# Two transformer blocks on one core: S5 mixer output by channel in 32-row products, a stacked phase table, other convolution taps, banks and end

## The chip, the core and the metric

The kernel runs on one core of a Trainium2 chip. The time of a run is the device time of one launch in microseconds (us). TensorE (PE) multiplies, VectorE (DVE), ScalarE (ACT) and GpSimd (POOL) do the rest, SyncE (SP) issues the DMAs of the one queue in use here. PSUM is the memory into which PE writes; SBUF is the memory from which it reads.

## The reference, cut to what matters

Two blocks on 512 positions of width 1024. The first has an S5 state-space mixer, whose output goes through GELU and a gated linear unit, beside an attention mixer (called nsa), then a feed-forward part. The second has two more mixers and a feed-forward part with a 3x3 depthwise convolution; a last root-mean-square norm ends it.

```python
# S5 mixer: 32 groups of 16 channels, 64 complex states each
_, _, xr, xi = lax.associative_scan(combine, (a_seq_re, a_seq_im, bu_re, bu_im), axis=1)
y = (jnp.einsum('bsgp,gcp->bsgc', xr, c_re.astype(f32))
     - jnp.einsum('bsgp,gcp->bsgc', xi, c_im.astype(f32))
     + d_skip.astype(f32).reshape(SSM_GROUPS, SSM_GROUP) * ug).reshape(bsz, s, SSM_WIDTH)
yg = jax.nn.gelu(y)
out = yg * jax.nn.sigmoid(yg @ w_glu.astype(f32) + b_glu.astype(f32))
...
# second block's feed-forward part
u = _dwconv2d(h @ w_up, conv_w, rows, cols)
a, b = jnp.split(u, 2, axis=-1)
return (jax.nn.silu(a) * b) @ w_down
```

## The kernel before

**Products.** Every large fp32 product is made of three products of rounded halves (`mm3`, L210 to L212): high by high, high by low, low by high. A unit of a projection (`proj`) is a tile of 128 output rows by 512 positions, 24 matmuls for 1024 inputs, into one PSUM bank. ACT rounds a weight tile (`wh<-raw`), DVE or POOL makes its rest (`wl<-raw,wh`); buffers: raw 2, wh 3, wl 3.

**PSUM.** Tags `mm` (4 banks), `aux` (3), `sm` (1). A unit waits until a bank of its tag has been read out.

**Order.** A scheduler orders each engine's instructions when the kernel is built; on the chip each engine takes its own queue strictly in that order, and waits at an instruction whose inputs, bank or buffer are not there.

**S5.** The first four units of the first projection (the last is `ps_mm_275`) give the mixer's input, which goes through `uv` and 32 small DMAs into `ur`. The next 16 units (gates, `gt`) don't depend on the mixer: they are what PE can do while DVE computes it. `s5_half` runs for halves hf 0 and 1, each over two channel tiles jt (0, 1 and 2, 3):
- `products` forms s5A, s5B (input weights) and s5CAr, s5CAi (output weights) on DVE; PE transposes s5A and s5B (L696), ACT copies the result into s5W1r and s5W1i.
- Powers of the decay (the phases s5Pr, s5Pi) are made by doubling, up to 127 of them in 7 steps.
- L705, L706 and L709 make the kernel of the first four lags (s5KT, s5G); POOL adds the skip term, 10 DMAs spread it.
- L733 multiplies `ur` by s5W1; DVE turns the result by the phases, scans (L757), turns back (s5Xr, s5Xi).
- L770 and L772 give `py` (`ps_sm`): position by channel, four blocks. To come back to channel by position, hf 0 goes through ACT and 16 DMAs; jt 2 takes 16 ACT operations of 32 rows; jt 3 takes 8 of these, 8 DVE copies (L794) and one ACT operation. `yg` is the GELU's result, ysH and ysL its halves, the input of `glu`.

After `glu` follow nsa's projections. In nsa, L1097 and L1099 give scores, L1119 transposes, L1055 and L1137 serve the coarse branch (cX).

**Second feed-forward part.** `ffn2` projects 44 units. The first four run together (banks mm); `conv_psum` reads each unit from its bank: ACT makes the middle tap (caccf) and one more (ctapf), DVE adds seven taps one after the other, POOL adds ctapf. The bank is free after the last DVE tap. Units 4 to 21 have their wl from POOL.

**End.** The last eight units (wdn2c) update x; squares (nsq, ACT) are summed (nacc, DVE), summed over rows (L366), rv, rr (POOL), rdg (DVE), spread (L382), and 16 DVE operations write y, which 8 DMAs store; for positions 0 to 255 and then for 256 to 511.

Of the kernel before, what the change touches and what calls it, by code (L numbers as in the profile page):

```python
# [179 lines left out]
class Kern:  # L180
# [63 lines left out]
    def proj(self, aps, xs, cb, kt=8, first=0, le=None, order=None, tail=0, mid=None, halves=False,  # L244
             pre={}, mid0=None, mid_at=-2):
# [66 lines left out]
    def sumsq(self, x, tmp, sl, tags=("nsq", "nacc")):  # L312
        n = sl.stop - sl.start
        acc = None
        for k in range(8):
            sq = tmp.tile([128, n], F32, name="nsq", tag=tags[0], bufs=2)
            self.act(sq, x[k][:, sl], AF.Square)
            if acc is None:
                acc = sq
            else:  # L320
                a2 = tmp.tile([128, n], F32, name="nacc", tag=tags[1], bufs=2)
                self.tt(a2, acc, sq, OP.add)
                acc = a2
# [33 lines left out]
    def rstd(self, acc, n, width, root=False, between=None):  # L357
# [3 lines left out]
        pin = self.tc.keep_in_program_order if between else lambda i: i  # L361
        between = between or (lambda n: None)
        nb = n // 128
        ss = self.mmtile((128, 8), "sm")
        for j in range(nb):
            self.ss_turn = nc.tensor.matmul(ss[:, j:j + 1], acc[:, 128 * j:128 * j + 128], self.ones[:, :1], start=True,  # L366
                                            stop=True).ins.name
        between(2)
        v = self.sm.tile([128, 4], F32, name="rv", tag="rv", bufs=2)
        pin(self.ts(v[:, :nb], ss[:, :nb], 1.0 / width, OP.mult, EPS, OP.add))  # L370
# [7 lines left out]
        between(2)  # L378
        pin(self.tt(dg[:, :n].rearrange("p (b t) -> p b t", b=nb), self.ident[:, None, :].to_broadcast([128, nb, 128]),
                    r[:, :nb, None].to_broadcast([128, nb, 128]), OP.mult))  # L380
        rb = self.mmtile((128, 512), "mm" if root else "aux")
        nc.tensor.matmul(rb[:, :n], self.ones, dg[:, :n], start=True, stop=True)  # L382
        between(8)
# [204 lines left out]
    def s5(self, hp, p, hs, prm, xs, pre):  # L588
# [5 lines left out]
        uv1 = lambda: uv()[:, 0]  # L594
# [7 lines left out]
        def norm():  # L602
            r, self.rt = self.rstd(self.sumsq(xs, hp, full, ("yg", "glus")), T, D, root=True)
# [18 lines left out]
    def s5_half(self, hp, hf, A, Gp, m4, u4, s5d, ura, uv1):  # L622
# [16 lines left out]
        def products(o, g, x, last):  # L639
# [4 lines left out]
            for c in range(2):  # L644
                nc.gpsimd.memset(o[c], 0.0)
                U = tile([128, 8, 4, 16], "s5t", 1)
                V = self.mmtile((128, 512), "aux")
                self.tt(U, gb[0], xb[c], mul)
                self.tt(V.rearrange("p (a l c) -> p a l c", a=8, l=4), gb[1], xb[1 - c], mul)
# [12 lines left out]
        P = [tile([128, 8, 128], n) for n in ("s5Pr", "s5Pi")]  # L662
        nc.gpsimd.memset(P[0][:, :, 0:1], 1.0)
        nc.gpsimd.memset(P[1][:, :, 0:1], 0.0)
        self.ts(P[0][:, :, 1], u4[0][:, ps], 1.0, mul)
        self.ts(P[1][:, :, 1], u4[1][:, ps], 1.0, mul)
        n = 1
        while n < 128:

            m = min(n, 127 - n)  # L670
            if m > 0:
                sr = P[0][:, :, n:n + 1].to_broadcast([128, 8, m])
                si = P[1][:, :, n:n + 1].to_broadcast([128, 8, m])
                xr, xi = P[0][:, :, 1:m + 1], P[1][:, :, 1:m + 1]
                orr, oi = P[0][:, :, n + 1:n + m + 1], P[1][:, :, n + 1:n + m + 1]
# [50 lines left out]
        for jt in (2 * hf, 2 * hf + 1):  # L726
            ur = ura[:, jt]
            q4 = slice(4 * (jt % 2), 4 * (jt % 2) + 4)
            wr = self.mmtile((128, 512), "aux")
            wi = self.mmtile((128, 512), "aux")  # L730
# [69 lines left out]
    def glu(self):  # L800
# [16 lines left out]
        for k in range(4):  # L817
            y = ys[k // 2][:, k % 2]
# [830 lines left out]
    def conv_psum(self, ps, w, pool, tag, bufs, tbufs):  # L1649
# [17 lines left out]
        self.tt(av[:, 1:8], av[:, 1:8], tv[:, 0:7], OP.add, nc.gpsimd)  # L1667
# [427 lines left out]
```

## Time and profile before

| what | value |
|---|---|
| median of 3 runs | 1656.02 us (1654.74 to 1656.45) |
| the profiled execution | 1655.87 us |
| its span, first to last instruction | 1654.2 us |
| mean granted clock of PE | 0.973 of full speed |
| busy in the span: PE, DVE, ACT, POOL | 1571.7, 1155.2, 733.0, 399.6 us |

Shares of the span are averages over stages that wait for different things; what counts for an engine is where it waits. A busy PE may run at half speed: the granted clock tells. Half of full speed is 1.2 GHz, full speed 2.4 GHz.

### The profile page before, as it was taken

Reading aid. Unit: us, or ns where it says so; the run is one execution under the profiler, and the core shown is the slowest. Engines: PE = TensorE matmul, PEld = TensorE weight load, DVE = VectorE, ACT = ScalarE, POOL = GpSimd, SP = SyncE. Lnnn points to the kernel's source line nnn. Section 1 sums busy time; section 2 is a strip of 40 time slices with the busy share of each in tenths; the row PEclk is TensorE's granted clock in tenths of the full one; section 3 lists DMA queues with packets and bytes.
Section 4 is the critical chain, followed back from the end, with each engine's and each line's share of the span. In section 5 each row is a group of like instructions: output and inputs, shape, how many; then the busy total and the mean of one; then the engine's idle time right before and its main releaser. Section 6 shows DMA issues by size and latency. Waiting matters only on the chain.

```text
span 1654.2 us, 22302 instructions
## 1 busy us (share of the span) xinstructions
PE 1571.7 (95%) x8277; PEld 1308.7 (79%) x8277; DVE 1155.2 (70%) x2209; ACT 733.0 (44%) x1286; POOL 399.6 (24%) x355
## 2 busy tenths in 40 slices
PE   7998898899999999999999999989989899999997
PEld 5887676677898888888887888878879788888886
DVE  8988625675769854863538888577868798777755
ACT  4354426553444213352335555556554454343422
POOL 1100203222100000000012222315220566656552
PEclk9999897999999999999999999999999899999998
DMA  5331310003346763733212011111212223233322
GB/s 178 105 96 47 124 59 26 14 20 98 126 166 206 249 218 110 250 124 102 83 64 65 26 39 52 59 52 51 77 52 69 72 94 102 90 102 91 101 86 80
DMA packets 60268, 158.34 MB, mean 96 GB/s; under 512 B 12416, under 2 KB 20352, under 8 KB 60032
## 3 DMA queue, kind: packets, MB, share of 16 engines
q1 hardware_dynamic: 60160, 156.92, 29.9%
q8 instruction: 65, 1.06, 0.3%
q14 instruction: 43, 0.35, 0.1%
HBM read 152.57 MB, written 2.10 MB: 94 GB/s over the span
## 4 chain that ended last, share of the span: by engine, by line
PE 73%; DVE 10%; ACT 5%; issue 2%; POOL 1%; DMA 0%; POOLq 0%; DVEq 0%; ACTq 0%
PE ps_mm L210 21%; PE ps_mm L211 21%; PE ps_mm L212 21%; PE ps_sm L1130 2%; PE ps_mm L1119 1%; DVE caccm L200 1%; DVE wl L191 1%; ACT L188 1%; DVE hgE L191 1%; PE ps_aux L1573 1%; DVE caccf L200 1%; PE ps_aux L1097 1%; ACT wh L188 0%; PE ps_mm L1007 0%; DVE hgl L1486 0%
## 5 line engine op out<-in xcount | busy, mean ns | idle before, releaser
L188 ACT ACTIVATE wh<-raw 128x1024 fp32r<-128x1024 f32 (+3 forms) x234 | 236.7, 1012 | 536.2 <-PE ps_mm L211 415.7
L191 DVE TENSOR_TENSOR wl<-raw,wh 128x1024 fp32r<-128x1024 f32 (+2 forms) x162 | 198.0, 1223 | 115.3 <-ACT wh L188 108.2
L200 DVE SCALAR_TENSOR_TENSOR caccf<-ps_mm,cwf,caccf 128x441 f32<-128x441 f32 (+2 forms) x308 | 206.7, 694 | 34.5 <-ACT ctapf L188 28.8
L191 POOL TENSOR_TENSOR wl<-raw,wh 128x1024 fp32r<-128x1024 f32 (+2 forms) x72 | 159.8, 2221 | 168.0 <-ACT wh L188 167.1
L210 PE MATMUL ps_mm<-h4H,wh 128*128 128x512 f32 (+1 forms) x368 | 137.0, 380 | 7.8 <-DVE caccf L200 7.6
L212 PE MATMUL ps_mm<-h4H,wl 128*128 128x512 f32 (+1 forms) x368 | 138.3, 378 | 0.0
L211 PE MATMUL ps_mm<-h4L,wh 128*128 128x512 f32 (+1 forms) x368 | 138.3, 379 | 0.0
L191 POOL TENSOR_TENSOR rr<-rv,nhalf 128x2 f32<-128x2 f32 x9 | 8.7, 968 | 435.0 <-DVE rv L197 435.0
L210 PE MATMUL ps_mm<-h2H,wh 128*128 128x512 f32 (+1 forms) x280 | 103.8, 372 | 0.0
L212 PE MATMUL ps_mm<-h2H,wl 128*128 128x512 f32 (+1 forms) x280 | 103.6, 371 | 0.0
L211 PE MATMUL ps_mm<-h2L,wh 128*128 128x512 f32 (+1 forms) x280 | 103.6, 371 | 0.0
L210 PE MATMUL ps_mm<-aH,wh 128*128 128x512 f32 (+1 forms) x272 | 102.6, 377 | 0.5 <-DVE x L191 0.5
L212 PE MATMUL ps_mm<-aH,wl 128*128 128x512 f32 (+1 forms) x272 | 102.7, 378 | 0.0
L211 PE MATMUL ps_mm<-aL,wh 128*128 128x512 f32 (+1 forms) x272 | 102.4, 377 | 0.0
L210 PE MATMUL ps_mm<-hH,wh 128*128 128x512 f32 x224 | 89.5, 406 | 9.6 <-ACT hH L188 8.9
L1265 DVE CUSTOM_DVE_ANT_0 msc<-wmod,cB,cols 128x1024 bf16<-128x1024 f32 x64 | 82.0, 1281 | 21.2 <-DMA wmod<-in_wmod 20.8
L211 PE MATMUL ps_mm<-hL,wh 128*128 128x512 f32 x224 | 90.1, 403 | 0.0
L212 PE MATMUL ps_mm<-hH,wl 128*128 128x512 f32 x224 | 89.4, 400 | 0.0
L210 PEld LDWEIGHTS ps_mm<-h4H,wh 128*128 128x128 f32 x368 | 68.7, 190 | 21.1 <-issue 7.7
L211 PEld LDWEIGHTS ps_mm<-h4L,wh 128*128 128x128 f32 x368 | 69.9, 190 | 13.2 <-DVE h4L L200 0.4
L212 PEld LDWEIGHTS ps_mm<-h4H,wl 128*128 128x128 f32 x368 | 69.8, 190 | 13.1
L210 PE MATMUL ps_mm<-faH,wh 128*128 128x512 f32 (+1 forms) x194 | 72.4, 373 | 0.0
(521 smaller groups left out, 4040.9 us busy)
## 6 DMA issues: line engine op xcount, KB each, us to landing
raw<-in_wup SPq DMA_DIRECT2D x76, 512.0 KB, 3.4
wmod<-in_wmod SPq DMA_DIRECT2D x48, 512.0 KB, 4.3
raw<-in_wdn SPq DMA_DIRECT2D x32, 512.0 KB, 3.5
raw<-in_win SPq DMA_DIRECT2D x28, 512.0 KB, 3.4
raw<-in_wout SPq DMA_DIRECT2D x8, 512.0 KB, 3.4
raw<-in_wdn2a SPq DMA_DIRECT2D x8, 512.0 KB, 3.4
raw<-in_wdn2b SPq DMA_DIRECT2D x8, 512.0 KB, 3.4
raw<-in_wdn2c SPq DMA_DIRECT2D x8, 384.0 KB, 3.0
```

Of the source, the lines that this page charges most:

```text
L188: return self.nc.scalar.activation(o, i, f, **k)
L191: return (e or self.nc.vector).tensor_tensor(o, a, b, op)
L200: return self.nc.vector.scalar_tensor_tensor(o, a, s, b, op0, op1)
L210: mm(ps, wh, xh, start=start, stop=False)
L211: mm(ps, wh, xl, start=False, stop=False)
L212: mm(ps, wl, xh, start=False, stop=stop)
L1097: nc.tensor.matmul(S[:, :n2], self.qs[:, 2 * j + g, c], self.ks[:, 2 * br + g, :n2], start=True, stop=False)
L1119: nc.tensor.transpose(tp[:, 128 * b:128 * b + 128], P[g, i][:, 128 * b:128 * b + 128], self.ident)
L1130: nc.tensor.matmul(O[64 * g:64 * g + 64, 128 * i:128 * i + 128], self.V[:, b, c:c + 64], PT[g][:, 128 * b:128 * b + 128], start=br == 0 an ...
L1265: ins = nc.vector.tensor_tensor_reduce(sc, w, cB[:, c], 1.0, bm[:, m:m + 1], OP.mult, OP.add, acc)
L1573: nc.tensor.matmul(ps[:, j], EE[:, li, 128 * j:128 * j + 128], vw(EE[:, li])[:, j], start=True, stop=True)
```

## The change

The mixer, the second feed-forward part and the end are written in another way; no weight layout changes.

1. **S5.** In `products` the last operation is one DVE instruction of 128 rows into PSUM, and ACT copies it out in two 64-row halves (before: two DVE instructions of 64 rows). The phases stand in one tile s5P, real and imaginary side by side, and a doubling step takes 4 DVE instructions, two of them of double width, instead of 6. The wr and wi of odd jt take `mm` banks instead of `aux`. The output `py` is made by 48 products of 32 rows per jt, four side by side (`tile_position`), instead of 12 of 128 rows; it comes out by channel, and one ACT operation makes yg. The copies and 32 DMAs behind it are gone.
2. **Second feed-forward part.** Units 0 to 17 have two taps on ACT and POOL and six on DVE. Units 4 and 5 get a bank of aux and the bank of sm.
3. **End.** wdn2c runs as 5 + 3 units; the squares of x tiles 0 to 4 are summed ahead of the last three, and L366's successor sums two accumulators. Of y, two tiles of eight are made by ACT and POOL.

```diff
-            ps = self.mmtile()
+            ps = self.mmtile(tag=banks[i - first] if i - first < len(banks) else "mm")
...
+                last[c](V, U, V)
                 for h in range(2):
                     r = slice(64 * h, 64 * h + 64)
-                    d = o[c][r, :, :, 16 * h:16 * h + 16].rearrange("p a l c -> p (a l) c")
-                    u = U[r].rearrange("p a l c -> p (a l) c")
-                    v = V[r].rearrange("p (n c) -> p n c", c=16)
-                    last[c](d, u, v)
+                    self.act(o[c][r, :, :, 16 * h:16 * h + 16].rearrange("p a l c -> p (a l) c"),
+                             V[r].rearrange("p (n c) -> p n c", c=16))
...
-                t = tile([128, 8, 64], "s5pt")[:, :, :m]
-                self.tt(t, xi, si, mul)
-                self.tt(orr, xr, sr, mul)
-                self.tt(orr, orr, t, sub)
-                t = tile([128, 8, 64], "s5pt")[:, :, :m]
-                self.tt(t, xi, sr, mul)
-                self.tt(oi, xr, si, mul)
-                self.tt(oi, oi, t, add)
+                by = lambda c: PP[:, c:c + 1, :, n:n + 1].to_broadcast([128, 2, 8, m])
+                x, o = PP[:, :, :, 1:m + 1], PP[:, :, :, n + 1:n + m + 1]
+                t = tile([128, 2, 8, 64], "s5pt")[:, :, :, :m]
+                self.tt(o, x, by(0), mul)
+                self.tt(t, x, by(1), mul)
+                self.tt(o[:, 0], o[:, 0], t[:, 1], sub)
+                self.tt(o[:, 1], o[:, 1], t[:, 0], add)
...
-            wr = self.mmtile((128, 512), "aux")
-            wi = self.mmtile((128, 512), "aux")
+            wr, wi = (self.mmtile((128, 512), ("aux", "mm")[jt % 2]) for _ in range(2))
...
-            for pl in range(4):
-                o = py[:, 128 * pl:128 * pl + 128]
-                pr = q4.start + pl
-                nc.tensor.matmul(o, G[:, pr].rearrange("p a b -> p (a b)"), ur[:, pl], start=True, stop=False)
-                for c in range(2):
-                    nc.tensor.matmul(o, CA[c][:, pr].rearrange("p a b -> p (a b)"), X[c][:, pl, 0:128],
-                                     start=False, stop=c == 1)
+            for st in range(4):
+                for i, (w, x) in enumerate(((G, ur), (CA[0], X[0]), (CA[1], X[1]))):
+                    for pl in range(4):
+                        nc.tensor.matmul(py[32 * pl:32 * pl + 32, 128 * st:128 * st + 128], w[:, q4.start + pl, st],
+                                         x[:, pl, 0:128], start=i == 0, stop=i == 2, tile_position=(0, 32 * pl))
...
+            self.act(yg.rearrange("p (c s) -> p s c", s=4), py.rearrange("p (s c) -> p s c", s=4), AF.Gelu_apprx_tanh)
...
-        self.act(tv[:, 0:7], rv[:, 0:7], scale=w[:, 1:2])
-        for dy, dx in ((1, 0), (0, -1), (0, 1), (-1, -1), (-1, 1), (1, -1), (1, 1)):
+        taps = ((0, -1), (0, 1), (-1, -1), (-1, 1), (1, -1), (1, 1), (1, 0), (-1, 0))
+        late = []
+        for i in range(8 - n_pool, 8):
...
+            self.act(g(t)[:, iy], rv[:, iy], scale=w[:, c:c + 1])
...
+        for dy, dx in taps[:8 - n_pool]:
...
+        for oy, t in late:
+            self.tt(av[:, oy], av[:, oy], t, OP.add, nc.gpsimd)
...
-                conv[m] = self.conv_psum(ps, cw[:, m // 2 + 22 * (m % 2)], p, "f", 8, 6)
+                conv[m] = self.conv_psum(ps, cw[:, m // 2 + 22 * (m % 2)], p, "f", 8, 6, 2 if m < 2 * lead else 1)
...
+                      banks=("aux", "sm"),
...
-            down("wdn2c", list(range(8)), 16, 6, tail=3, mid=lambda: rb.append(self.norm_factor(self.x, p, h0)))
+            down("wdn2c", list(range(5)), 16, 6)
+            for i, sl in enumerate((h0, h1)):
+                early.append(self.sumsq(self.x, p, sl, tags=("nsq", f"nacc{i}"), tiles=range(5)))
+            down("wdn2c", [5, 6, 7], 16, 6, tail=3, mid=mid)
```

In the changed kernel L687 is the transposes of s5A and s5B (before L696), L696, L697 and L700 the kernel of the first lags (before L705, L706, L709), L723 the product with `ur` (before L733), L761 the products for `py` (before L770, L772), L1101 the transposes of cX (before L1137). The order on PE, as built, moves in three places.

**PE behind the fourth unit `ps_mm_275`.** Before, two gate units (770, 803) stand between it and the first transposes of S5:

```order
L212 MATMUL ps_mm_275<-hH_78,wl_272 128x512
L210 MATMUL ps_mm_770<-hH_78,wh_766 128x512
...
L212 MATMUL ps_mm_803<-hH_78,wl_800 128x512
L696 MATMUL ps_aux_536<-ident_76,s5A_438 128x128 x4
L210 MATMUL ps_mm_803<-hH_78,wh_799 128x512
```

With the change, transposes, products with `ur` and the lag kernel come first, and the first gate unit is 786:

```order
L212 MATMUL ps_mm_275<-hH_78,wl_272 128x512
L687 MATMUL ps_aux_518<-ident_76,s5A_438 128x128 x4
L687 MATMUL ps_aux_524<-ident_76,s5A_438 128x128 x4
L687 MATMUL ps_aux_530<-ident_76,s5B_439 128x128 x4
L687 MATMUL ps_aux_536<-ident_76,s5B_439 128x128 x4
L723 MATMUL ps_mm_675<-ur_123,s5W1r_516 128x128 x4
L696 MATMUL ps_aux_543<-s5A_438,s5c_432 32x128
...
L697 MATMUL ps_aux_556<-s5B_439,s5nci_496 32x128
L723 MATMUL ps_mm_676<-ur_123,s5W1i_517 128x128 x4
L210 MATMUL ps_mm_786<-hH_78,wh_782 128x512
```

45 matmuls of gate units have moved from before the first transposes to behind the lag kernel.

**PE at the end of S5.** Before, the outputs of jt 3 (`ps_sm_1304`) come after the last gate unit (1575), among those of `glu` (1620 to 1622):

```order
L212 MATMUL ps_mm_1575<-hH_78,wl_1572 128x512
L210 MATMUL ps_mm_1620<-ysH_83,wh_1604 128x512
...
L770 MATMUL ps_sm_1304<-ur_123,s5G_1188 128x128
...
L772 MATMUL ps_sm_1304<-s5Xi_1295,s5CAi_1115 128x128
L210 MATMUL ps_mm_1620<-ysH_83,wh_1604 128x512
```

With the change, jt 3 (`ps_sm_1323`) comes inside gate unit 1547, with two more gate units (1580, 1613) behind it and ahead of `glu` (1659):

```order
L212 MATMUL ps_mm_1547<-hH_78,wl_1544 128x512
L761 MATMUL ps_sm_1323<-ur_123,s5G_1186 32x128 x4
L761 MATMUL ps_sm_1323<-s5Xr_1313,s5CAr_1110 32x128 x4
L761 MATMUL ps_sm_1323<-s5Xi_1314,s5CAi_1111 32x128 x4
...
L210 MATMUL ps_mm_1547<-hH_78,wh_1543 128x512
...
L210 MATMUL ps_mm_1580<-hH_78,wh_1576 128x512
...
L210 MATMUL ps_mm_1613<-hH_78,wh_1609 128x512
...
L210 MATMUL ps_mm_1659<-ysH_83,wh_1643 128x512
```

Gate units have moved from ahead of the outputs of jt 3 to behind them.

**PE at the start of the second feed-forward part.** Before, unit 4 (11530, an mm bank) follows the first four:

```order
L212 MATMUL ps_mm_11244<-h4H_10840,preL_11234 128x256
...
L210 MATMUL ps_mm_11530<-h4H_10840,wh_11526 128x512
...
L210 MATMUL ps_mm_11580<-h4H_10840,wh_11576 128x512
```

With the change, unit 5 (`ps_sm_11627`) follows them, then unit 6 in an mm bank, then unit 4 (`ps_aux_11575`):

```order
L212 MATMUL ps_mm_11281<-h4H_10877,preL_11271 128x256
L210 MATMUL ps_sm_11627<-h4H_10877,wh_11623 128x512
...
L210 MATMUL ps_mm_11672<-h4H_10877,wh_11668 128x512
...
L210 MATMUL ps_aux_11575<-h4H_10877,wh_11571 128x512
...
L210 MATMUL ps_mm_11724<-h4H_10877,wh_11720 128x512
```

The first unit behind the first four no longer shares a bank with them.

## Rows read from the trace of the kernel before

**Rows 1.** Waits of PE: what for, us, times, longest.
```profile
PE ps_mm L210 <- DVE caccf L200: 7.6, 1, 7.6
PE ps_mm L210 <- ACT ysH L188: 7.5, 1, 7.5
PE ps_aux L1137 <- DVE cX L191: 4.8, 1, 4.8
```

**Rows 2.** Windows over S5: length, busy PE PEld DVE ACT POOL, granted clock, DMA.
```profile
40.00:150.00 110.00, 110.00 (x621) 92.04 (x621) 99.33 (x201) 44.43 (x63) 12.22 (x21) 1.00 0.31 89
150.00:160.00 10.00, 8.36 (x31) 6.21 (x30) 7.08 (x17) 9.62 (x19) 0.00 (x0) 0.86 0.16 52
160.00:170.00 10.00, 5.68 (x28) 4.90 (x26) 4.69 (x8) 1.50 (x4) 0.00 (x0) 0.80 0.00 0
170.00:180.00 10.00, 4.08 (x10) 3.21 (x11) 4.38 (x11) 5.26 (x10) 0.00 (x0) 0.54 0.00 0
```

**Rows 3.** Timeline of PE and ACT, end of S5: start, us, [idle before <-releaser].
```profile
149.01 6.41 ACT L188 ACTIVATE yg<-ps_sm 32x128 f32<-32x128 f32 x16 [2.31 <-PE ps_sm L772]
155.47 0.49 PE L770 MATMUL ps_sm<-ur,s5G 128*128 128x128 f32 x2 [1.48 <-ACT yg L188]
164.24 0.76 PE L772 MATMUL ps_sm<-s5Xr,s5CAr 128*128 128x128 f32 x2 [2.75 <-DVE s5Xr L191]
168.47 3.17 ACT L188 ACTIVATE yg<-ps_sm 32x128 f32<-32x128 f32 x8 [8.64 <-PE ps_sm L772]
175.92 1.65 PE L210 MATMUL ps_mm<-ysH,wh 128*128 128x512 f32 x3 [7.49 <-ACT ysH L188]
```

**Rows 4.** Timeline of DVE and ACT after the fourth unit.
```profile
40.98 1.06 ACT L188 ACTIVATE wh<-raw 128x1024 fp32r<-128x1024 f32 x1 [7.70 <-PE ps_mm L211]
43.89 1.06 DVE L191 TENSOR_TENSOR uv<-ps_mm,rbs 128x512 f32<-128x512 f32 x1
47.44 1.37 DVE L191 TENSOR_TENSOR s5CAr<-s5t,ps_aux 64x512 f32<-64x512 f32 x2
51.80 0.60 ACT L188 ACTIVATE s5W1r<-ps_aux 128x512 f32<-128x512 f32 x1 [1.37 <-PE ps_aux L696]
```

**Rows 5.** Timeline of PE around products of 32 rows, and of 128x512.
```profile
57.86 0.45 PE L705 MATMUL ps_aux<-s5A,s5c 128*32 128x128 f32 x8
58.10 0.42 PE L706 MATMUL ps_aux<-s5B,s5nci 128*32 128x128 f32 x8
58.45 0.50 PE L210 MATMUL ps_mm<-hH,wh 128*128 128x512 f32 x1
58.80 0.40 PE L211 MATMUL ps_mm<-hL,wh 128*128 128x512 f32 x1
59.03 0.40 PE L212 MATMUL ps_mm<-hH,wl 128*128 128x512 f32 x1
```

**Rows 6.** DVE instructions by form, 60 to 150 us: busy, mean ns, idle before.
```profile
L191 DVE TENSOR_TENSOR wl<-raw,wh 128x1024 fp32r<-128x1024 f32 x12 | 14.7, 1223 | 1.8 <-ACT wh L188 1.8
```

**Rows 7.** Window behind PE's wait for cX in nsa, columns as in rows 2.
```profile
300.00:310.00 10.00, 8.49 (x45) 6.95 (x45) 6.08 (x21) 4.72 (x15) 2.52 (x1) 0.66 0.01 2
```

**Rows 8.** Second feed-forward part: DVE taps, POOL (min/median/max ns), windows as in rows 2.
```profile
1288.16 17.26 DVE L200 SCALAR_TENSOR_TENSOR caccf<-ps_mm,cwf,caccf 128x448 f32<-128x448 f32 x28 [5.75 <-ACT ctapf L188]
1287.10 4.75 POOL L191 TENSOR_TENSOR wl<-raw,wh 128x1024 fp32r<-128x1024 f32 x2 [14.87 <-ACT wh L188]
L191 POOL TENSOR_TENSOR caccf<-caccf,ctapf x22: 1145/1156/1167, 1298.5 to 1413.7; 128x448 f32<-128x448 f32 x22
1300.00:1305.00 5.00, 5.00 (x15) 3.96 (x14) 5.00 (x10) 0.26 (x1) 1.24 (x2) 0.60 0.00 0
1320.00:1340.00 20.00, 20.00 (x90) 16.57 (x89) 18.70 (x30) 8.95 (x14) 12.51 (x8) 1.00 0.34 105
```

**Rows 9.** End: the last sum of squares on PE, y on DVE.
```profile
1643.46 0.58 PE L366 MATMUL ps_sm<-ones,nacc 128*128 128x1 f32 x4 [1.63 <-DVE nacc L191]
1645.38 4.79 DVE L200 SCALAR_TENSOR_TENSOR y<-x,cols,ps_aux 128x256 f32<-128x256 f32 x12
```

More of the change, by code (lines that the diff above doesn't have):

```diff
@@ L309, in bact, with sumsq @@
         return ins
-    def sumsq(self, x, tmp, sl, tags=("nsq", "nacc")):
+    def sumsq(self, x, tmp, sl, tags=("nsq", "nacc"), tiles=range(8), acc=None):
         n = sl.stop - sl.start
-        acc = None
-        for k in range(8):
+        for k in tiles:
             sq = tmp.tile([128, n], F32, name="nsq", tag=tags[0], bufs=2)
@@ L365, in rstd @@
         for j in range(nb):
-            self.ss_turn = nc.tensor.matmul(ss[:, j:j + 1], acc[:, 128 * j:128 * j + 128], self.ones[:, :1], start=True,
-                                            stop=True).ins.name
-        between(2)
+            for i, acc in enumerate(accs):
+                self.ss_turn = nc.tensor.matmul(ss[:, j:j + 1], acc[:, 128 * j:128 * j + 128], self.ones[:, :1],
+                                                start=i == 0, stop=i == len(accs) - 1).ins.name
         v = self.sm.tile([128, 4], F32, name="rv", tag="rv", bufs=2)
-        pin(self.ts(v[:, :nb], ss[:, :nb], 1.0 / width, OP.mult, EPS, OP.add))
+        self.ts(v[:, :nb], ss[:, :nb], 1.0 / width, OP.mult, EPS, OP.add)
         r = self.sm.tile([128, 4], F32, name="rr", tag="rr", bufs=2)
@@ L659, in s5_half @@
         products(T1, Gp, bc[:, 0:2], (minus, lambda d, u, v: self.tt(d, u, v, add)))
-        P = [tile([128, 8, 128], n) for n in ("s5Pr", "s5Pi")]
+        PP = tile([128, 2, 8, 128], "s5P")
+        P = [PP[:, 0], PP[:, 1]]
         nc.gpsimd.memset(P[0][:, :, 0:1], 1.0)
         nc.gpsimd.memset(P[1][:, :, 0:1], 0.0)
-        self.ts(P[0][:, :, 1], u4[0][:, ps], 1.0, mul)
-        self.ts(P[1][:, :, 1], u4[1][:, ps], 1.0, mul)
+        for c in range(2):
+            self.ts(P[c][:, :, 1], u4[c][:, ps], 1.0, mul)
         n = 1
@@ L2051, in ffn2 @@
             fin = self.col2("fin")
-            def store(sl, rb):
-                for k in range(8):
-                    if k % 2 == 0:
-                        y = p.tile([128, 2, 256], F32, name="y", tag="faH", bufs=17)
-                    self.tc.keep_in_program_order(
-                        self.stt(y[:, k % 2], self.x[k][:, sl], fin[:, k:k + 1], rb, mul, mul))
-                    if k % 2:
-                        nc.sync.dma_start(self.out[k - 1:k + 1, :, sl].rearrange("k p n -> p k n"), y)
-                    yield
@@ L2063, in between @@
-            def between(n):
-                for _ in zip(range(n), s0):
-                    pass
-            rb = []
-            h0, h1 = slice(0, 256), slice(256, 512)
-            down("wdn2c", list(range(8)), 16, 6, tail=3, mid=lambda: rb.append(self.norm_factor(self.x, p, h0)))
-            s0 = store(h0, rb[0])
-            r1 = self.rstd(self.sumsq(self.x, p, h1), 256, D, between=between)[0]
-            for _ in store(h1, r1):
-                pass
+            h0, h1 = slice(0, 256), slice(256, 512)
@@ new lines, in factor @@
+            def factor(sl, acc):
+                acc = self.sumsq(self.x, p, sl, tiles=(5, 6), acc=acc)
+                sq = p.tile([128, 256], F32, name="nsq", tag="nsq", bufs=2)
+                self.act(sq, self.x[7][:, sl], AF.Square)
+                return self.rstd([acc, sq], 256, D)[0]
+            def store(sl, rb):
+                y2 = p.tile([128, 2, 256], F32, name="y", tag="faH", bufs=17)
+                for i in range(2):
+                    self.act(y2[:, i], self.x[6 + i][:, sl], scale=fin[:, 6 + i:7 + i])
+                rbs = p.tile([128, 256], F32, name="rbl", tag="rbl", bufs=2)
+                self.act(rbs, rb)
+                for i in range(2):
+                    self.tt(y2[:, i], y2[:, i], rbs, mul, nc.gpsimd)
+                for k in range(0, 6, 2):
+                    y = p.tile([128, 2, 256], F32, name="y", tag="faH", bufs=17)
+                    for i in range(2):
+                        self.stt(y[:, i], self.x[k + i][:, sl], fin[:, k + i:k + i + 1], rb, mul, mul)
+                    nc.sync.dma_start(self.out[k:k + 2, :, sl].rearrange("k p n -> p k n"), y)
+                nc.sync.dma_start(self.out[6:8, :, sl].rearrange("k p n -> p k n"), y2)
@@ L2076, in build, with mid @@
+            early, rb = [], []
+            def mid():
+                rb.append(factor(h0, early[0]))
+            down("wdn2c", list(range(5)), 16, 6)
+            for i, sl in enumerate((h0, h1)):
+                early.append(self.sumsq(self.x, p, sl, tags=("nsq", f"nacc{i}"), tiles=range(5)))
+            down("wdn2c", [5, 6, 7], 16, 6, tail=3, mid=mid)
+            r1 = factor(h1, early[1])
+            store(h0, rb[0])
+            store(h1, r1)
 def build(tc, I, out, dbg=None, stop=99):
```

76 lines of the change are left out of this document (23 added, 53 removed).

## The prediction, made before the changed kernel was run

> **What bounds the kernel now.** I read the waits of PE first: of its idle time three waits fall to places that the change touches, 7.6 us for the convolution of the second feed-forward part, 7.5 us for ysH at the end of S5 and 4.8 us for cX in nsa [rows 1]. Then the windows, since idle time is not all: behind a wait the granted clock stands at its lower level. In 40 to 150 us PE has no gap, at full clock, with DVE busy 99.33 of 110 us [rows 2]; there only more work on PE, or a PE queue that waits, can cost. In 150 to 180 us PE is busy 8.36, 5.68 and 4.08 of three times 10 us: 11.9 us are idle. The mean clocks of 0.86, 0.80 and 0.54 mean 2.8, 4.0 and 9.2 us at half speed; PE worked in all of the first two and in 4.08 us of the third, so about 1.4, 2.0 and 2.0 us are lost, together 5.4 us. So 17.3 us go there. The chain behind it: 16 small ACT operations for jt 2, 6.41 us; PE idle 1.48 us for them, then 2.75 us for DVE; 8 more ACT operations, DVE copies, one more ACT operation; and PE idle 7.49 us until ysH [rows 3].
>
> **The end of S5.** The change takes out this chain. In the new order, gate units 1580 and 1613 and a part of 1547 stand behind the last product for jt 3, ahead of glu. A unit is 24 matmuls at 0.23 us start to start [rows 5], 5.4 us, so over 14 us of work cover one ACT operation for yg (under 2 us, by the 6.41 us of sixteen, a bound from above) and its rounding. The 17.3 us go, if DVE is in time with s5X of jt 3. By the DVE queue it is: with 0.62 us for an instruction of 128x512 (17.26 us for 28 [rows 8]) and about 1.2 us for a wl [rows 6], I walked the queue and came to about 140 us for s5X of jt 3, where PE still has some 20 us of gates. The 32 DMAs that go from SP's queue were waited for by ACT's yg of hf 0 alone, under gates that keep PE full to 150 us [rows 2]; I cost them at nothing.
>
> **The start of S5: a new wait.** This speaks against the change. PE ends its fourth unit at 40.9 (ACT takes its weight buffer at 40.98 [rows 4]). Before, 45 gate matmuls follow; now the transposes do. The first of them takes the aux bank that held the sum for s5CAr: its order waits for DVE's last step and for ACT's copies out of it. Before, DVE reaches uv at 43.89 and has s5CAr at 47.44 + 1.37 = 48.8 [rows 4]. In the new queue the same steps and one wl stand ahead, with a 128-row step in place of the pair and wider phase steps; I get 48.6. Two ACT copies of at most 0.60 us each [rows 4] make 49.7. PE idles from 40.9 to 49.7. Behind it four transposes, each followed by an ACT copy of 0.60 us before its bank serves again, then the lag kernel and 8 products with ur, at half clock: the first gate matmul at about 54.9. Of these 14.0 us some 4.4 us is work that before stood elsewhere (two lag kernels of 0.59 us [rows 5], 16 transposes at about 0.09 and 16 half-products at 0.11 us, a quarter of a 128x512 one with two passes). Loss 9.6 us, and 1.2 us more until the clock is back: 10.8 us. Bounds: 6 us, if the scheduler's bank is free earlier than I read, and 14 us, if the clock stays low through the mixed work as it does for 9.2 us in 170 to 180 [rows 2]. Queued behind PE's wait are all gates, whose weights are there, and the first products with ur for DVE, which so waits about 2.5 us and can make it up; the lag kernel's ten DMAs for s5G come earlier than before, and PE asks for them a gate unit later.
>
> **Smaller waits and the products.** In hf 1 the same block of transposes stands without gates in between; its inputs are there, and the copies cost about 1.7 us. While jt 1 and jt 3 hold two of the four mm banks, a gate unit waits until DVE has read the last but one: I find 0.3 and 1.5 us. Together 3.5 us, 0 to 6. For py, 48 products make 96 records per jt against 24 before. Sixteen 32-row records took 0.59 us, from 57.86 to 58.45, the first eight 0.24 us [rows 5]: 30 to 37 ns each, 2.9 to 3.5 us per jt, against 24 times 0.11 = 2.7. I take 0.45 us more each, 1.8 us for four.
>
> The Trainium skill (TensorEngine Tiling (Array Packing), Key Properties) says that tiles side by side work in parallel but that changing the tiling mode drains TensorE. The row agrees in size: the 0.35 us from the second eight to the next 128x512 matmul is 0.11 us more than the first eight took; by the rule some ten changes would add 1 us to the sum, which lies inside the bounds.
>
> S5 in sum: -17.3 + 10.8 + 3.5 + 1.8 = -1.2; the glu matmuls now run at full clock for another 0.5 us at 180 us, and fewer changes between small and large products save about 0.8: **-2.5 us**, from -9 to +4.
>
> **Nsa, not edited but reordered.** With another start the scheduler pulls cX forward on DVE: its subtraction now follows its reduction directly, and PE has four gate matmuls and all scores ahead of L1101. The 4.8 us [rows 1] shrink to about 1 by the same durations. Behind it the clock was 0.66 in 300 to 310 [rows 7], 6.8 us at half, some 2.9 us lost. But DVE must then still scale the scores, so I take **-3 us**, of 0 to -7.
>
> **Second feed-forward part.** PE waits 7.6 us for the first bank and then runs at half clock for 1.5 us and 4 us (0.60 in a window of 5 us [rows 8]), 2.7 us lost: 10.3 us. Now unit 5 starts in bank sm at once. It needs POOL's wl: POOL starts at 1287.10, 2.4 us each [rows 8], so the second ends at 1291.9, and PE waits about 0.6 us. While it runs (5.4 us), DVE frees the bank of unit 0: six taps of 0.62 us per unit. Then unit 6, unit 4 (aux), 7. Per unit POOL has 2.4 + 2 times 1.16 = 4.7 us and DVE about 4.3 against PE's 5.4, so neither falls behind; I allow 0.7 us of small waits. **-9 us**, of -4 to -10.3.
>
> ACT gets one tap of some 0.6 us per unit more and was busy 8.95 of 20 us [rows 8]: covered. The first DVE tap now waits for two ACT taps; behind it stand only taps of the same unit, and the cover is the 1.1 us per unit that DVE has spare. Without it: 0.6 us a unit.
>
> The Trainium skill (SBUF — State Buffer, SBUF: two separate sides) says that GpSimd and a DVE instruction with two SBUF inputs lock each other out of a shared port for a whole instruction. The trace does not show it here: the POOL adds took 1145 to 1167 ns in 22 cases, beside a DVE that was busy 18.70 of 20 us [rows 8], with taps that read PSUM. [...]
>
> **End.** L366 starts at 1643.46 and y runs from 1645.38 for 4.79 us on DVE, twelve instructions [rows 9]. With the sums of five tiles made ahead, the last sum is ready about 1 us earlier; of 16 y's four go to ACT and POOL, two of them in the last half, some 0.8 us less on DVE; but six y of the first half now stand in DVE's queue ahead of rv. **-1 us**, 0 to -2.
>
> **Sum.** -2.5 - 3 - 9 - 1 = -15.5, against the profiled execution: 1655.87 - 15.5 = 1640.4. That execution lies 0.15 us under the median of 1656.02. I predict 1640 us.
>
> **Rivals.**
> *The early wait eats more than the end gives.* PE has no cover at 41 us, and with 14 us lost, 6 us of bank waits, and nothing from nsa, S5 is 4 us dearer; with 8 us from the second feed-forward part and 1 from the end the time is 1651. For it: mixed small products keep the clock low in 170 to 180 us. Against: gates are dense from 55 us on. Chance 0.17.
> *The 32-row products run one after the other (the other side).* If each record took the 0.11 us of a 128-row one, a jt would need 10.6 us, 7.9 more, and four of them 31 us: 1671 us less the 1.8 counted, about 1670. It decides from 37 + 15500 / 384 = 77 ns a record. Against: the sixteen records of 30 to 37 ns have the same form. For: those 16 are a short burst, with positions of another operand. Chance 0.05.
> *The feed-forward stall moves to POOL.* If each of the two adds waits for one tap of 0.62 us, POOL needs 5.9 us a unit, 0.5 more than PE, over 14 units 7 us: the time would be 1647. [...] Against: 1145 to 1167 ns. Chance 0.10.
> *The early bank comes free sooner or nsa gives all.* 6 us instead of 10.8 and -7 in nsa: 1631. Chance 0.13.
> The forecast itself, 1635 to 1646, has 0.50; the remaining 0.05 is a small gain or none, 1652 to 1660.
>
> **How the numbers follow.** A measurement of this kernel can tell about 0.2% (3.3 us) from no change. Faster than 1652.7: 0.50, 0.10, 0.13 and most of 0.17, with 0.02 of the rest: 0.90. Within 0.2%: 0.04. Slower: 0.06, the serial products and a worse start. The range holds the forecast, the early wait, POOL and most of the better case: 1630 to 1651 us.
>
> **What would show it.** Right: PE idle for about 9 us from 40.9 us on, with transposes as the next work and a half clock; no wait of PE from 140 us to glu; records of 32 rows some 30 to 37 ns apart; a wait of under 1 us behind the first four feed-forward units; the wait for cX under 2 us. Wrong: a full PE at 41 to 50 us (then the time is near 1630), idle PE at glu, POOL without gaps in 1300 to 1380 us, or 0.11 us between 32-row records.

## The result, and the profile after

The changed kernel took 1636.91 us (median of 4 runs, 1635.24 to 1638.55) against 1656.13 us for the kernel before, run beside it: a ratio of 0.9886, 95% interval 0.9868 to 0.9903. The profiled execution took 1638.55 us with a span of 1636.8 us, 17.3 us less than before's; 15.5 us were forecast. The page of the changed kernel:

```profile
PE 1567.7 (96%) x8573; PEld 1302.8 (80%) x8573; DVE 1130.2 (69%) x2141; ACT 746.1 (46%) x1301; POOL 418.0 (26%) x377
```

The shares have hardly moved. Its waits of PE (us, times, longest) have:

```profile
PE ps_aux L687 <- DVE s5t L191: 8.9, 1, 8.9
...
PE ps_aux L379 <- DVE rdg L191: 2.6, 1, 2.6
...
PE ps_aux L1101 <- DVE cX L191: 1.2, 1, 1.2
...
PE ps_sm L212 <- POOL wl L191: 0.7, 1, 0.7
...
PE ps_mm L210 <- DVE caccf L200: 0.4, 1, 0.4
```

Against [rows 1]: the 7.6 us for caccf are 0.4, and 0.7 for POOL's wl; the 7.5 us for ysH are gone; cX fell from 4.8 to 1.2; and there is one new wait of 8.9 us, for s5t. Windows of the changed kernel, columns as in [rows 2]:

```profile
28.00:38.00 10.00, 7.36 (x18) 4.57 (x17) 10.00 (x63) 1.67 (x3) 0.00 (x0) 0.68 0.31 107
...
40.00:50.00 10.00, 1.40 (x7) 0.81 (x5) 10.00 (x21) 4.40 (x7) 0.00 (x0) 0.76 0.21 53
50.00:60.00 10.00, 9.70 (x80) 8.78 (x81) 5.25 (x8) 4.49 (x10) 1.67 (x3) 0.73 0.29 86
...
40.00:150.00 110.00, 100.25 (x774) 81.68 (x773) 95.45 (x181) 50.81 (x71) 8.71 (x21) 0.95 0.26 78
150.00:160.00 10.00, 10.00 (x129) 8.29 (x128) 4.26 (x6) 7.51 (x9) 0.00 (x0) 1.00 0.10 28
160.00:170.00 10.00, 10.00 (x46) 8.29 (x45) 2.31 (x4) 2.64 (x5) 0.00 (x0) 1.00 0.18 52
170.00:180.00 10.00, 10.00 (x46) 8.29 (x45) 4.66 (x7) 5.46 (x9) 0.00 (x0) 1.00 0.50 158
...
290.00:300.00 10.00, 8.57 (x56) 5.75 (x55) 8.69 (x28) 6.07 (x17) 3.20 (x2) 1.00 0.09 26
300.00:310.00 10.00, 10.00 (x68) 6.98 (x67) 4.03 (x12) 4.64 (x14) 0.00 (x0) 1.00 0.00 0
...
1320.00:1340.00 20.00, 20.00 (x90) 16.49 (x89) 19.58 (x33) 13.48 (x22) 18.46 (x14) 1.00 0.31 104
```

From 150 us on PE is full at full clock, where [rows 2] had 8.36, 5.68 and 4.08 us of 10. The price stands in 40 to 60 us: PE busy 1.40 us in the first ten, and a clock of 0.76 and 0.73. In 300 to 310 us the clock is 1.00, not 0.66 [rows 7]. The timeline (start, us, [idle before <-releaser]):

```profile
50.30 1.94 PE L687 MATMUL ps_aux<-ident,s5A 128*128 128x128 f32 x8 [8.91 <-DVE s5t L191]
...
57.57 0.47 PE L210 MATMUL ps_mm<-hH,wh 128*128 128x512 f32 x1
...
151.29 0.39 PE L212 MATMUL ps_mm<-hH,wl 128*128 128x512 f32 x1
151.61 0.43 PE L761 MATMUL ps_sm<-ur,s5G 128*32 128x128 f32 x8
151.85 0.40 PE L761 MATMUL ps_sm<-s5Xr,s5CAr 128*32 128x128 f32 x8
...
154.03 0.41 PE L761 MATMUL ps_sm<-s5Xi,s5CAi 128*32 128x128 f32 x8
154.37 0.50 PE L210 MATMUL ps_mm<-hH,wh 128*128 128x512 f32 x1
...
154.50 1.07 ACT L188 ACTIVATE yg<-ps_sm 128x512 f32<-128x512 f32 x1 [0.75 <-PE ps_sm L761]
...
1283.07 0.50 PE L212 MATMUL ps_sm<-h4H,wl 128*128 128x512 f32 x1 [0.72 <-POOL wl L191]
...
1624.99 2.44 DVE L200 SCALAR_TENSOR_TENSOR y<-x,cols,ps_aux 128x256 f32<-128x256 f32 x6 [0.36 <-ACT rbl L188]
...
1628.79 1.11 PE L379 MATMUL ps_aux<-rdg,ones 128*128 128x256 f32 x2 [2.64 <-DVE rdg L191]
```

The products of jt 3 are twelve groups of eight 32-row records; from 151.61 to 154.03 us a group starts every 0.22 us. One ACT operation of 1.07 us stands where 16 and 8 stood [rows 3].

To compare whole kernels I cut each profiled execution at five matmuls of the timeline: the start of the fourth unit's last matmul; the end of glu's last product with ysL; the end of nsa's last product of probabilities and values; the end of the first four units of the second feed-forward part; and the last matmul into x. Durations in us:

```
                       start    S5    nsa  middle   ffn2   end   span
     before             40.7  142.4  210.1  897.7  350.5  12.8  1654.2
     changed            41.0  138.6  203.2  899.1  342.2  12.7  1636.8
e1   S5 alone           36.7  140.9  204.5  896.9  350.5  12.5  1642.0
e2   ffn2 alone         40.8  142.8  210.2  897.8  341.9  12.7  1646.2
e3   end alone          39.9  142.4  210.0  901.7  350.7  13.2  1657.9
e4   aux banks          37.1  132.4  215.7  897.8  342.3  12.4  1637.7
e5   mm for jt 3        40.6  141.6  208.3  897.6  342.2  12.4  1642.7
e6   old outputs        40.1  137.9  208.6  896.8  342.2  12.7  1638.3
e7   banks only         36.8  142.7  212.2  897.8  349.5  12.7  1651.7
e8   taps only          40.2  142.4  210.0  897.8  347.0  12.7  1650.1
e9   one mm, jt 3       40.3  140.0  207.4  899.4  342.3  12.3  1641.7
e10  two gates first    39.4  135.5  208.0  899.7  342.2  12.4  1637.2
e11  one gate first     40.2  135.2  204.9  896.8  342.2  12.3  1631.6
```

The changed kernel: S5 -3.8, nsa -6.9, ffn2 -8.3, middle +1.4, end 0. PE's part of the start, which no kernel here edits, spans 36.7 to 41.0 us, and the middle 896.8 to 901.7: differences of this size between two spans say nothing of an edit unless they stand in its own column. How far one program scatters can be read too: before, e2, e3, e7 and e8 run the same instructions in the same order up to 390 us, and their five profiles have 36.8 to 40.8 us for the start, 142.4 to 142.8 for S5 and 210.0 to 212.2 for nsa.

### The profile page after: what moved, and what is told of

It reads as the page before. It is cut to its first block, busy times and chain, and to the rows that moved or that the text cites. A ratio compares the mean times of both kernels' runs of the same rounds, so it can differ in the third digit from the quotient of the medians.

```text
span 1636.8 us, 22811 instructions
## 1 busy us (share of the span) xinstructions
PE 1567.7 (96%) x8573; PEld 1302.8 (80%) x8573; DVE 1130.2 (69%) x2141; ACT 746.1 (46%) x1301; POOL 418.0 (26%) x377
## 4 chain that ended last, share of the span: by engine, by line
PE 79%; DVE 13%; ACT 5%; issue 2%; POOL 1%; DMA 0%; SPq 0%; DVEq 0%; ACTq 0%
PE ps_mm L210 22%; PE ps_mm L211 22%; PE ps_mm L212 22%; PE ps_sm L1094 2%; DVE wl L191 2%; PE ps_mm L1083 1%; DVE caccm L200 1%; ACT L188 1%; DVE hgE L191 1%; PE ps_sm L761 1%; ACT wh L188 1%; PE ps_aux L1537 1%; DVE caccf L200 1%; PE ps_mm L971 0%; PE ps_aux L1061 0%
## 5 line engine op out<-in xcount | busy, mean ns | idle before, releaser
L200 DVE SCALAR_TENSOR_TENSOR caccf<-ps_mm,cwf,caccf 128x441 f32<-128x441 f32 (+2 forms) x278 | 188.5, 695 | 30.9 <-ACT ctapf L188 24.7
L212 PE MATMUL ps_mm<-h4H,wl 128*128 128x512 f32 (+1 forms) x352 | 131.2, 375 | 0.0
L211 PE MATMUL ps_mm<-h4L,wh 128*128 128x512 f32 (+1 forms) x352 | 131.1, 375 | 0.0
L210 PE MATMUL ps_mm<-h4H,wh 128*128 128x512 f32 (+1 forms) x352 | 129.7, 377 | 0.6 <-DVE caccf L200 0.4
L211 PEld LDWEIGHTS ps_mm<-h4L,wh 128*128 128x128 f32 x352 | 66.2, 188 | 12.3 <-DVE h4L L200 0.4
L212 PEld LDWEIGHTS ps_mm<-h4H,wl 128*128 128x128 f32 x352 | 66.2, 188 | 12.2
L210 PEld LDWEIGHTS ps_mm<-h4H,wh 128*128 128x128 f32 x352 | 65.0, 188 | 13.5 <-issue 0.8
```

The source lines that it names most:

```text
L200: return self.nc.vector.scalar_tensor_tensor(o, a, s, b, op0, op1)
L210: mm(ps, wh, xh, start=start, stop=False)
L211: mm(ps, wh, xl, start=False, stop=False)
L212: mm(ps, wl, xh, start=False, stop=stop)
```

## Experiments

Behind each time stands its ratio to the kernel before, run beside it, with the 95% interval.

**The three parts one by one.** Each part of the change alone in the kernel before.

```diff
 # e1: all S5 edits   e2: conv_psum with n_pool, banks=("aux", "sm")   e3: wdn2c as 5 + 3, sumsq early, y on three engines
```

> Before with the S5 part alone. Theory (the parts add up): S5 gives 3.5 us up to the first projection of nsa, with the 8.9 us wait of PE behind the fourth unit, and the reordered nsa gives 5 to 6 us more, so 1646 to 1648 us; the convolution still waits 7.6 us and the end is unchanged. Rival (nsa's part in the profile of after is only another phase of the clock): 1651 to 1653 us, with a wait for cX of over 3 us.

> Before with the second feed-forward part alone, banks and taps. Theory: PE's wait of 7.6 us falls to about 1 us and the half clock behind it goes, 7 to 8 us less, 1648 to 1649 us; S5 and nsa are as before. Rival (the gain of 7 us in the trace of after hangs on another place): 1653 us or more.

> Before with the end alone. Forecast in the prediction: 1 us less. After the result: from the last x to the end of y 8.65 us in after and 8.73 in before, so 0, within 0.1% of before.

S5 alone: 1644.02 us, 0.9931 (0.9915 to 0.9948). ffn2 alone: 1647.82, 0.9950 (0.9935 to 0.9965). The end alone: 1656.50, 1.0005 (0.9996 to 1.0015). Waits of PE with S5 alone, 40 to 395 us:

```profile
PE ps_aux L691 <- DVE s5t L191: 11.7, 1, 11.7
...
PE ps_aux L1105 <- DVE cX L191: 1.2, 1, 1.2
```

S5 alone brings the early wait and the small wait for cX together, so nsa's gain (-5.6 in its column) belongs to the S5 edits. The time lies under the 1646 to 1648 us expected, but its -12 us are flattered: 4.0 us of them lie in the start. Its windows:

```profile
28.00:38.00 10.00, 6.86 (x26) 4.72 (x26) 10.00 (x51) 1.00 (x2) 0.00 (x0) 1.00 0.23 70
```

The clock is 1.00 where the changed kernel has 0.68, though PE's instructions are the same in both up to there. That also explains why its early wait is longer: PE is there 4.3 us sooner, the first transposes only 1.6 us (48.7 against 50.3). ffn2 alone gives -8.6 in its own column and nothing elsewhere, as expected. The end gives nothing, as expected.

**Which edit covers the late waits?** First the mm banks of odd jt put back to aux; then the mm banks kept and the old outputs put back.

```diff
 # e4
-            wr, wi = (self.mmtile((128, 512), ("aux", "mm")[jt % 2]) for _ in range(2))
+            wr, wi = (self.mmtile((128, 512), "aux") for _ in range(2))
 # e6: py by 12 products of 128 rows, copies and DMAs as before
```

> The changed kernel with wr and wi of jt 1 and jt 3 in aux banks again, all else kept. In its order two gate units and more stand behind the fourth unit again, and the outputs of jt 3 stand among the products of glu, behind the last gate. Theory: the mm banks made both the early wait and the cover at the end. Then PE has no wait at 41 us, and waits at the end of S5 for s5X or ysH, 3 to 8 us and some half clock; against the changed kernel from -6 to +1 us. Rival (the early wait comes from products and the bank that s5CAr's sum holds): PE still waits over 5 us between 41 and 55 us.

> The changed kernel with the output of before: 12 products of 128 rows, DMAs for jt 0 and 1, small ACT and DVE operations for jt 2 and 3. Its order keeps two gate units behind jt 3's outputs. Theory A (the order of gates took away the waits at the end of S5): within 3 us of the changed kernel, no PE wait over 1 us from 130 to 180 us. Theory B (the output by channel took them away): PE waits again, 5 us or more, and the time is 6 to 12 us longer.

e4: 1639.77 us, 0.9908 (0.9893 to 0.9922). e6: 1640.07, 0.9906 (0.9893 to 0.9920). Waits of PE in e6, 40 to 350 us:

```profile
PE ps_aux L688 <- DVE s5t L191: 10.2, 1, 10.2
PE ps_aux L1126 <- DVE cX L191: 4.8, 1, 4.8
```

and its windows at the end of S5:

```profile
150.00:160.00 10.00, 10.00 (x58) 8.72 (x57) 3.59 (x6) 9.78 (x20) 0.00 (x0) 1.00 0.16 39
160.00:170.00 10.00, 10.00 (x46) 8.29 (x45) 5.73 (x14) 7.41 (x14) 0.00 (x0) 1.00 0.12 42
```

With all the old copies and DMAs PE is full there, and S5 is no longer than in the changed kernel (137.9 against 138.6): the gate units behind jt 3 take the late waits away by themselves, as theory A had it. The time is 3.2 us longer than the changed kernel's, a little over theory A's 3 us, because nsa's gain is lacking: the 4.8 us for cX are back. Waits of PE in e4, 40 to 350 us, then its windows at the end of S5:

```profile
PE ps_aux L859 <- ACT sq L188: 3.8, 1, 3.8
PE ps_aux L1101 <- DVE cX L191: 3.7, 1, 3.7
...
PE ps_sm L761 <- DVE s5Xr L191: 2.0, 1, 2.0
PE ps_mm L210 <- ACT ysH L188: 1.8, 1, 1.8
```

```profile
150.00:160.00 10.00, 7.99 (x79) 6.15 (x81) 10.00 (x21) 3.46 (x4) 0.00 (x0) 0.97 0.16 54
160.00:170.00 10.00, 8.17 (x75) 6.33 (x67) 3.55 (x6) 5.86 (x8) 0.00 (x0) 0.86 0.16 52
```

With aux banks the early wait is gone, so the mm banks made it and the rival is out. S5 falls to 132.4 us, though the last outputs have no gates behind them: with the output by channel that chain is short, and PE idles 3.8 us in these 20 us, where the kernel before has 6.0 in them and 5.9 in the ten behind [rows 2]. So each of the two, the gates behind jt 3 (e6) and the short chain (e4), takes most of the late waits away without the other. All that S5 wins and more goes in nsa, 12.5 us longer than in the changed kernel, with the waits for sq and cX and a stretch at half clock at each. The time is 2.9 us above the changed kernel's, where -6 to +1 was expected, and it is that near only since its start was 3.9 us shorter, with the clock at 1.00 in 28 to 38 us.

**Early gates and late gates at once.** Four ways to have both.

```diff
 # e5: mm banks for jt 3 only
+            wr, wi = (self.mmtile((128, 512), "mm" if jt == 3 else "aux") for _ in range(2))
 # e9: one mm bank, for wi of jt 3
+            wr, wi = (self.mmtile((128, 512), "mm" if jt == 3 and i else "aux") for i in range(2))
 # e10 (two gate units ahead of the first half of S5) and e11 (one: 1 for 2)
+        self.gates(hs, 0, 0, 2)
...
-        self.gates(hs, 0)
+        self.gates(hs, 0, 2, 8)
```

> The changed kernel with mm banks for wr and wi of jt 3 only, aux for jt 1. In its order the early gates are back and jt 3's outputs stand ahead of three gate units. Theory: no wait of PE at 41 us and none at the end of S5; 8.9 us idle and some 1 to 2 us of half clock less than the changed kernel, 1626 to 1629 us. Rival (the late cover was paid for with the early wait, so DVE is too late without it): a wait of some 5 us in the second block of transposes or before glu, 1631 to 1635 us.

> The changed kernel with only the wi of jt 3 taken from the mm banks (wr and wi of the other jt from aux). Theory A (the order of gates decides everything): the early wait of 8.9 us at 50 us and the half clock behind it go, since jt 1 no longer holds the banks that the first gates need; but as with mm for jt 3 alone, jt 1's outputs and second transposes stand without gates between them, so the waits at 100 to 112 us (5.9, 2.4 and 1.1 us there) come back. The order after S5 is like the changed kernel's, so the wait for cX stays near 1 us and S5's end to the last PTV takes some 203 us, not 209. Sum: 1637 to 1640, same as the changed kernel. Rival: with one bank less held, those waits shrink, and the time is 1627 to 1631.

> The changed kernel with the first two gate units issued ahead of the first half of S5 in the program; the mm banks stay for both odd jt. Theory A: the gates now lie between the s5t transforms and the second transposes of jt 0 and 1, so the early 8.9 us wait and the half clock behind it go, the gates behind jt 1 and jt 3 still cover the late ones, and S5 ends at 168 to 172 us instead of 179.6. The order after it is like that of the kernel before, so the wait for cX is again 3.5 to 5 us and some 5 to 7 us are given back between S5's end and the last PTV: 1630 to 1635. Rival: the two units issued early are missing behind a later jt, where a wait of 5 us or more opens with a stretch of half clock, and the time is 1637 or more.

> The changed kernel with one gate unit, not two, issued ahead of the first half of S5 in the program. Theory (the early wait is set by when DVE has s5t, and each gate unit ahead of the transposes takes its 5.4 us out of the wait): the wait for s5t falls from 8.9 to about 3.5 us, with some half clock behind it, and the rest of S5 is as in the changed kernel, so S5 ends near 174 to 176 us instead of 179.6. The order in nsa is neither that of the kernel before nor that of the changed one; by the runs so far PE's half clock behind cX comes with the idle time ahead of it: if PE idles under 1.5 us in the 10 us about cX the gain stays, and the time is 1631 to 1635; if it idles over 2 us, 3.4 to 6.8 us of half clock come behind it, and it is 1636 to 1641. Rival: the gate unit's place decides little, DVE is late later instead, S5 ends at 178 us or after, and the time is 1637 or more with no half clock in nsa.

e5: 1643.98 us, 0.9928 (0.9916 to 0.9940); my theory fell, and so did the time that the rival gave, though its wait came. Its waits of PE, 40 to 350 us:

```profile
PE ps_sm L761 <- DVE s5Xr L191: 5.9, 1, 5.9
PE ps_aux L1101 <- DVE cX L191: 3.7, 1, 3.7
...
PE ps_aux L687 <- DVE ps_aux L191: 2.4, 1, 2.4
```

The early wait is gone, but now jt 1's outputs and the second transposes stand bare at 100 to 112 us: 9.4 us of waits in place of 8.9, with more of PE's work at half clock, so that S5 is 3.0 us longer than in the changed kernel, and nsa 5.1. e9: 1638.33, 0.9896 (0.9879 to 0.9912), a time as expected; the 5.9 us are there again. Its windows about cX:

```profile
290.00:300.00 10.00, 7.85 (x48) 5.26 (x48) 8.30 (x22) 4.88 (x13) 2.77 (x2) 1.00 0.09 28
300.00:310.00 10.00, 10.00 (x44) 6.99 (x44) 4.40 (x15) 3.93 (x12) 0.09 (x1) 0.66 0.00 0
```

Here the wait for cX is 0.7 us, yet the clock falls behind it, as it did before [rows 7]: the small waits ahead of it left PE 2.15 us idle in 290 to 300 us, and nsa takes 207.4 us, not some 203. This profile is of the longest of its five runs (1634.66 to 1643.37).

e10: 1639.92, 0.9905 (0.9890 to 0.9921). The early wait went, and S5 ended at 174.9 us, not at 168 to 172: the waits that took its place (PE, 40 to 190 us) are

```profile
PE ps_aux L688 <- ACT s5CAi L188: 4.0, 2, 2.5
PE ps_aux L688 <- ACT s5W1r L188: 1.8, 1, 1.8
```

the longest at 105 us with half clock behind it, and nsa gave 4.8 us back. That is nearer to its rival, in several small waits instead of one of 5 us. e11: **1634.57**, 0.9873 (0.9856 to 0.9889), the lowest median of all. Waits of PE, 40 to 395 us, then windows of 290 to 310 us (cX is transposed at 288.57 us here, without a wait):

```profile
PE ps_aux L688 <- DVE s5P L191: 3.5, 1, 3.5
PE ps_aux L688 <- ACT s5W1r L188: 2.3, 2, 1.9
```

```profile
290.00:300.00 10.00, 8.88 (x52) 6.05 (x53) 8.17 (x27) 7.76 (x24) 2.25 (x2) 1.00 0.09 26
300.00:310.00 10.00, 10.00 (x82) 7.67 (x81) 7.88 (x26) 5.76 (x19) 2.85 (x2) 1.00 0.13 29
```

The wait ahead of the first transposes is now for s5P. One gate unit of 5.4 us took 5.4 us out of the 8.9, as the theory had it, and S5's column fell by 3.4 us; PE idles 1.12 us ahead of 300 us, the clock stays, and nsa keeps most of its gain. The intervals of e11 and of the changed kernel overlap, so that e11 is some 2 us faster is likely, not shown.

**Second feed-forward part, split.** Banks alone and taps alone in the kernel before.

> Before with aux and sm banks for units 4 and 5, seven taps on DVE. Theory: the banks give nearly all, PE's wait of 7.6 us falls under 2 us, 5 to 8 us less than before. Rival: seven taps a unit make DVE late, and PE waits 3 us or more in the units behind.

> Before with two taps on ACT and POOL, no extra banks. Theory: DVE frees the first mm bank after 24 taps' order instead of 28, so PE's wait falls from 7.6 to some 5 us and the clock still falls: 1 to 4 us less than before. Rival: taps alone give the gain, wait under 2 us, 6 us or more less.

e7: 1654.18 us, 0.9992 (0.9982 to 1.0001), not told from the kernel before; the theory fell, and the rival's wait came. e8: 1651.73, 0.9981 (0.9971 to 0.9992), as expected. Waits of PE, 1270 to 1340 us, of e7 and then of e8:

```profile
PE ps_mm L210 <- DVE caccf L200: 6.2, 2, 4.9
PE ps_sm L212 <- POOL wl L191: 0.5, 1, 0.5
```

```profile
PE ps_mm L210 <- DVE caccf L200: 4.0, 1, 4.0
```

In their own column they give -1.0 and -3.5, together (e2) -8.6. With banks alone unit 5 runs at once but DVE, at seven taps a unit, is late for the next ones; with taps alone the first bank comes sooner, but PE still waits for it, and its clock is 0.66 in 1290 to 1300 us. Each takes away a wait that the other would leave.

## Why the prediction was right, step by step

The time follows from three quantities of PE in a stretch: idle time, half of its busy time at half clock (what that clock costs), and the rest, its own work. In the column of S5 these are, in us: before 11.88, 5.84 and 124.7; changed 9.75, 2.55 and 126.3; old outputs (e6) 11.69, 1.76 and 124.4.

**End of S5: -17.3, right, and for the reasons given.** Both of them: e6 shows that gate units behind jt 3 are enough, e4 that the short chain alone leaves some 4 us idle. DVE began s5Xr of jt 3 at 146.36 us, not at about 140, and glu starts at 168.78, so that the gates had enough to spare.

**The early wait: right in place, too small in sum.** Idle was 8.91 us where 8.8 were worked out; the first gate unit starts at 57.57, not 54.9. By the windows PE lost 8.9 idle, and of about 5 us of work at half clock half, 2.6: 11.5 against 10.8. What spoke for a clock that stays low was misread: in 170 to 180 us PE stood idle up to 175.92 and then ran 128x512 products of glu [rows 3], not mixed small ones.

**Smaller waits, 3.5: too large.** In 40 to 150 us PE idles 9.75 us, 8.91 of it the early wait: 0.8.

**32-row products, 1.8: about 1.9, but not where I had put it.** The burst that I sized them by had 30 to 37 ns a record; inside a block it is 0.22 / 8 = 27. In e6 the old products (those of jt 3 stand below) start two every 0.22 us, 0.11 us each, so four 32-row records side by side take the time of one of 128 rows:

```profile
154.93 0.39 PE L210 MATMUL ps_mm<-hH,wh 128*128 128x512 f32 x1
155.16 0.38 PE L762 MATMUL ps_sm<-ur,s5G 128*128 128x128 f32 x2
...
157.61 0.39 PE L764 MATMUL ps_sm<-s5Xi,s5CAi 128*128 128x128 f32 x2
157.75 0.48 PE L211 MATMUL ps_mm<-hL,wh 128*128 128x512 f32 x1
```

Serial products, a rival, are out. The cost stands at the edges of a block. From the last 128x512 product to the first small one it is 0.32 us in the changed kernel (151.29 to 151.61) and 0.23 here; from the last group to the next 128x512 one 0.34 (154.03 to 154.37) and 0.14. That is 0.29 us a block, and the seven blocks of 32-row products in the changed kernel make 2.0 us. PE's own work says the same: 126.3 us against 124.4 in e6. So the size of the term was luck. The Trainium skill (TensorEngine Tiling (Array Packing), Key Properties) has such tiles in parallel, and the trace agrees. It also has a drain at a change of mode; the 0.29 us a block stand where that would show, where I had read 0.11 us from one row, but whether the drain or the loading of the small weights makes them is not shown.

S5 in sum came out at -3.8 for a forecast of -2.5: -17.7 + 11.5 + 0.8 + 1.6, where 17.7 has the half clock up to 181 us in it, and 1.6 is the work, 1.9 for the products less 0.3 where 0.8 was forecast. The errors partly cancel.

**Nsa, -3: the term that was furthest off.** Measured -6.9, inside the bounds of 0 to -7; one program's nsa scatters by 2 us. The row of the wait (4.8 to 1.2) and the clock behind it (0.66 to 1.00, some 2.9 us) add up to 6.5; both were in the text, and I took less because DVE must still scale the scores. The other waits of PE in nsa did not grow to make up for it (for mn 3.0 to 3.5 us, for qs 2.1 to 1.9).

**Second feed-forward part, -9: -8.3.** The wait for POOL's wl is 0.72 us, forecast 0.6. Idle time and half clock give 9.2 us less; PE's own work there is 1.0 us more, which I can't place. The rival with POOL is out; this row of the changed kernel (min/median/max ns) answers to [rows 8]:

```profile
L191 POOL TENSOR_TENSOR caccf<-caccf,ctapf x42: 1142/1156/1172, 1287.8 to 1412.4; 128x448 f32<-128x448 f32 x42
```

The adds kept their 1156 ns beside a DVE busy 19.58 of 20 us, though POOL now has 18.46 of 20: it has hardly anything spare. The lock that the Trainium skill (SBUF — State Buffer, SBUF: two separate sides) describes for a DVE instruction with two SBUF inputs does not show in these adds; of a tap's two tensors one lies in PSUM.

**End, -1: nothing.** The chain after the last matmul takes 12.7 us against 12.8: six y of the first half stand at 1624.99 for 2.44 us in DVE's queue, ahead of the second half's rv, as the text said they would, and PE waits 2.64 us for rdg.

**The sum.** -17.3 us of span for a forecast of -15.5. Nsa gave 3.9 us more than forecast and S5 1.3; the second feed-forward part gave 0.7 less, the end 1 less, and the middle, which no edit touches, was 1.4 longer. The mechanisms hold place by place, but that the sum came so near is in part luck.

## What to carry to other kernels

A stall can be moved to where it is cheaper, and the order of independent work (here gate units of 5.4 us) can do what an edit of the operations was meant to do: with all the old output operations put back, S5 took 137.9 us against 138.6. Ask for each wait which independent work stands ahead of it and which behind. An edit that changes a scheduler's start changes the order in parts nobody touched; nsa, unedited, took from 203 to 216 us here, so read every stage, not the edited one alone. Small products of another tile size cost at the edges of each block, 0.29 us here, not inside it; that fewer blocks would cost less was not tested. Where a bank and a slow reader cause one wait together, try both edits at once: alone they gave 1.0 and 3.5 us, together 8.6.

## What was not expected of the hardware

**The start.** The same instructions of PE ended at 36.7 to 41.0 us. The rows differ in the granted clock: 1.00 in 28 to 38 us with S5 alone, with aux banks and with banks only, 0.68 in the changed kernel, 0.66 before. Banks only (e7) is up to there the program of before, so its 36.8 us against 40.7 are no property of a kernel; what decides it stays open.

**The clock behind cX.** PE's idle time in 290 to 300 us and the clock of 300 to 310: before 3.29 us and 0.66; e9 2.15 and 0.66; changed 1.43 and 1.00; S5 alone 1.44 and 1.00; e11 1.12 and 1.00, with cX transposed at 288.57 us already. In e4, e5, e6 and e10 PE idles 3.67, 3.70, 4.79 and 2.52 us in 290 to 300 us, and the clock falls within it, to means of 0.66, 0.87, 0.66 and 0.83. Waits that differ by a microsecond so came to differ by some 4 us. That the idle time is the cause was not tested by itself.
